# S5 powers advanced on inputs and outputs by one operation, and half of the memory's keys moved between the scan's gate and the merge

## The chip, the cores and the metric

The kernel runs on one core of one Trainium2 chip. The metric is device microseconds of one execution. A profiled execution stands beside the timed ones; its rows tell when each instruction of each engine began, how long it took and what ended the idle time before it.

## The reference, cut to what matters

Two layers of a trunk: three mixers side by side (S5, latent attention, HGRN2), their merge, attention to a memory, an FFN. x is 256 x 1024, the memory has 256 rows.

```python
h = rmsnorm(x, norm_mix[l])
(u_ssm, q_lat, kv_lat, k_rope, hg_q, hg_f, hg_i, hg_g, gate_logits) = split(h @ w_in[l])
y_ssm = s5_mixer(u_ssm, ...)        # B = ((exp(lam*step)-1)/lam) * b;  s_t = lam_bar*s_(t-1) + B u_t
                                    # y = gelu(Re(C s_t) + d*u);  z_out, z_gate = split(y @ w_glu)
                                    # return z_out * sigmoid(z_gate)
y_mla = mla_mixer(...);  y_hg = hgrn2_mixer(...)      # hgrn2 uses bounds: cumsum of softmax(hg_lb)
gates = sigmoid(gate_logits)
merged = gates[0]*y_ssm + gates[1]*y_mla + gates[2]*y_hg
x = x + merged @ w_out[l]
k, v = split(rmsnorm(mem, norm_mem[l]) @ x_w_kv[l])   # the memory's keys and values
x = x + softmax((rmsnorm(x, norm_cross[l]) @ w_q) k^T) v @ w_o
x = x + swiglu_ffn(rmsnorm(x, norm_ffn[l]))           # 1024 -> 2 x 2816 -> 1024
```

## The kernel before

Activations lie transposed, a tile of 128 rows for each of eight column groups k, with the 256 positions beside one another. Every weight chunk of up to 1 MB is fetched by SP (`raw`), then split in two for TensorE: ACT writes the rounded part `wH`, DVE the remainder `wL` (each 128x1024, two a chunk). Activations are split the same way (`h` for the input, `m` for the merged branches, `ex` for the memory, `yx` for the S5 output). Three raw buffers and four pairs of splits go round. A product is made of matmuls with wH (256 or 512 wide) and with wL.

The program is written as coroutines that a pacing loop interleaves: `LATS` says by layer how much work of a coroutine is let in beside a matmul, and `Plan` replays the whole order once, to give each tile one of the slots of `SLOTS` (t4 tiles are 4 KB a row, t2 and t1 smaller; a smaller kind may fall back on a larger slot). Each engine then runs its instructions in the fixed order that comes out, and SP its DMAs.

Five places matter.

- **Start.** `first()` makes the first input's products column group by group, with ACT and DVE splitting h and the weights as they land. POOL adds the squares for the norm beside them (L659), `col_sums` sums them over partitions, `finish` makes the row factor R, and DVE scales the four S5 inputs (`Ue`). `hg_bounds` (L669 to 693) makes the HGRN2 bounds `hb` by a chain of small DVE operations on 128x4.
- **Powers.** `s5_powers` (L816 to 852) makes the input side times lam^0..3 (`Q`) and the output side times lam^0..4 (`Pw`, `P4`), each power by six DVE operations on 128x256. Layer 0's run early in the mixers, layer 1's in layer 0's FFN.
- **S5 core.** `s5_main` (L856 to 975) does two halves: Gp and G from Q, the small matrix Tm (from tm, by DMA), products `b`, two rotations, the scan (L931), the states `X`, then y = Tm Ush + Cp X. It runs between attention heads (S, Ssb, PT, oT) and the gates (`gt`).
- **Scan to merge.** `scan(i)` makes the two halves of the gated output for 512 columns each (`zg` the gate, `zo` the value), multiplies with the branch gates (mu, Tg), and transposes Tg by TensorE (`mT`, L1415). `upd` then multiplies m with w_out and adds to x.
- **After the merge.** The memory's keys `Kc` are made from `ex` in two halves of 256 columns (`halves` makes 16 pairs of matmuls, 512 and 256 wide), followed by the query's products, which need the new x, normed and split, for all eight column groups. `drain` ends the coroutine that loads and splits the memory (`mT`, `mnat`, 0.5 MB each, L1148 and L1152; ACT squares mnat into `junk`).

Of the kernel before, what the change touches and what calls it, by code (L numbers as in the profile page):

```python
# [100 lines left out]
SLOTS = dict(t4=23, t2=10, t1=4, tn=8, tk=8, ps=8)  # L101

LEAD = 2
LATS = (0.9, 1.7)
# [13 lines left out]
class Plan:  # L118
# [40 lines left out]
def trunk(ctx, tc, A, out, plan):  # L159
# [59 lines left out]
    def tt(o, a, b, op):  # L219
        dve(o)  # L220
        DVE.tensor_tensor(out=o, in0=a, in1=b, op=op)  # L221
# [261 lines left out]
    def build_chunks(l):  # L483
        C = {}
# [28 lines left out]
        C["xk"] = [wcols(A["x_w_kv"][l], 0, 8, 256 * i, 256) for i in range(2)]  # L513
# [68 lines left out]
    def col_sums(s, ps=None):  # L582

        ps = ps if ps is not None else bank("ms")[:, 0:2]
        for tt_ in range(2):
            mm(ps[:, tt_:tt_ + 1], s[:, tt_ * 128:tt_ * 128 + 128], ones)
# [55 lines left out]
    def first(k):  # L642
# [11 lines left out]
        else:  # L654
# [14 lines left out]
    def hg_bounds():  # L669
# [3 lines left out]
        tt(lmx, gcol[:, lo:lo + 4], gcol[:, lo + 4:lo + 8], ALU.max)  # L673
# [142 lines left out]
    def s5_powers(l, bc_=None):  # L816

        ls = slice(16 * l, 16 * l + 16)
# [6 lines left out]
        S5Q[l] = (Q, Pw, P4)  # L825
        yield

        def bc(v):
            return v[:, ls].unsqueeze(2).to_broadcast([128, 16, 16])

        def cmul(o, a, b, conj=False):

            pl, mi = (ALU.subtract, ALU.add) if conj else (ALU.add, ALU.subtract)
            p1, p2 = t1([16, 16], F32, "cm"), t1([16, 16], F32, "cm")
            tt(p1, bc(a[:, 0]), b[0], ALU.mult)
            tt(p2, bc(a[:, 1]), b[1], ALU.mult)
            tt(o[0], p1, p2, mi)
            p3, p4 = t1([16, 16], F32, "cm"), t1([16, 16], F32, "cm")
            tt(p3, bc(a[:, 0]), b[1], ALU.mult)
            tt(p4, bc(a[:, 1]), b[0], ALU.mult)  # L840
            tt(o[1], p3, p4, pl)
        cmul([q[:, 3] for q in Q], coef, B)
        yield
        for k in range(1, 4):
            cmul([q[:, 3 - k] for q in Q], lam, [q[:, 4 - k] for q in Q])
            yield
        for n in range(2):
            acopy(Pw[n][:, 0], bc_[:, 2 + n], scale=-1.0 if n else None)
        yield
        for d in range(1, 5):  # L850
            cmul([q[:, d] for q in Pw] if d < 4 else P4, lam, [q[:, d - 1] for q in Pw], conj=True)
            yield

    sp = ctx.enter_context(tc.tile_pool(name="sp", bufs=1))

    def s5_main(l, Ush, out_y, heads):  # L856
        Q, Pw, P4 = S5Q.pop(l)
        gm = [cf[:, CG:CG + 1], cf[:, CG + 1:CG + 2]]
        for hf in range(2):
# [6 lines left out]
            for n in range(2):  # L866
                for g2 in range(2):
                    acopy(Gp[n][:, :, :, g2, :].rearrange("p i k h -> p k i h"), Q[n][:, :, i0:i0 + 8, :], scale=gm[g2])
# [30 lines left out]
            for i in range(8):  # L899

                for n in range(2):
                    mm(ps[0:32, 64 * i:64 * i + 64], Gp[n][:, i, 3].rearrange("p b c -> p (b c)"),
                       Pw[n][:, :, i0 + i, :], start=n == 0, stop=n == 1)
# [282 lines left out]
    def layer(l, nrm):  # L1186
# [23 lines left out]
        if l == 0:  # L1210
            nrm.sums = col_sums(sq0[0][:, 0])
# [177 lines left out]
        def scan(i):  # L1389
            zg, zo = [[bank(n) for _ in range(2)] for n in ("zg", "zo")]  # L1390

            def half(n, ps, k):
                for tt_ in range(2):
                    projB(C[n, i, k], range(2), 0, 512, ps[tt_], yHL, tt_, kbase=k, first=k == 0, last=k == 2)
# [12 lines left out]
            half("zo", zo, 2)  # L1407
            tps = [bank("mT") for _ in range(2)]
# [13 lines left out]
        ex = []  # L1422
# [226 lines left out]
```

## Time and profile before

| | us |
|---|---|
| median of 3 timed runs | 1093.5 (1093.49 to 1094.94) |
| profiled execution | 1094.6 |
| its span, first to last instruction | 1092.8 |
| TensorE busy | 1072.5 (98%) |
| VectorE (DVE) busy | 829.1 (76%) |
| ScalarE (ACT) busy | 636.4 (58%) |
| GpSimd (POOL) busy | 37.7 (3%) |
| TensorE idle while waiting for another engine | 14.0 |
| mean granted TensorE clock, as a share of full speed | 0.992 |

Busy time is the sum of an engine's instructions. TensorE is all but full, so time is to be had in its idle stretches and in the stretches where it ran at half clock; the other engines count where TensorE waits for them.

### The profile page before, as it was taken

Reading aid. Unit: us, or ns where it says so; the run is one execution under the profiler, and the core shown is the slowest. Engines: PE = TensorE matmul, PEld = TensorE weight load, DVE = VectorE, ACT = ScalarE, POOL = GpSimd, SP = SyncE. Lnnn points to the kernel's source line nnn. Section 1 sums busy time; section 2 is a strip of 40 time slices with the busy share of each in tenths; the row PEclk is TensorE's granted clock in tenths of the full one; section 3 lists DMA queues with packets and bytes.
Section 4 is the critical chain, followed back from the end, with each engine's and each line's share of the span. In section 5 each row is a group of like instructions: output and inputs, shape, how many; then the busy total and the mean of one; then the engine's idle time right before and its main releaser. Section 6 shows DMA issues by size and latency. Waiting matters only on the chain.

```text
span 1092.8 us, 16654 instructions
## 1 busy us (share of the span) xinstructions
PE 1072.5 (98%) x6416; PEld 938.0 (86%) x6416; DVE 829.1 (76%) x1438; ACT 636.4 (58%) x1050; POOL 37.7 (3%) x52
## 2 busy tenths in 40 slices
PE   8999999989899999999999999999999999999997
PEld 8999888878688888888888899888888888888887
DVE  7996777786687789986768887767677868887753
ACT  6645756855455566564565447965545566555542
POOL 4001000000000000000010001000000000000000
PEclk9999999989899999999999999999999999999999
DMA  8745552342655455655656442543474535655551
GB/s 292 214 117 178 176 163 82 116 148 85 204 167 181 133 195 193 193 183 183 188 181 186 121 136 78 191 130 108 163 233 148 197 123 167 194 191 193 174 190 61
DMA packets 145024, 179.08 MB, mean 164 GB/s; under 512 B 13553, under 2 KB 108657, under 8 KB 144945
## 3 DMA queue, kind: packets, MB, share of 16 engines
q1 hardware_dynamic: 144512, 177.45, 50.6%
q8 instruction: 50, 0.82, 0.3%
q10 hardware_dynamic: 432, 0.57, 0.2%
q14 instruction: 30, 0.24, 0.1%
HBM read 174.59 MB, written 1.05 MB: 161 GB/s over the span
## 4 chain that ended last, share of the span: by engine, by line
PE 72%; ACT 1%; DVE 0%; issue 0%; POOLq 0%; POOL 0%; ACTq 0%
PE hv L213 32%; PE dn L213 11%; PE quad L213 6%; PE gt L213 6%; PE xv L213 2%; PE ho L213 1%; PE mo L213 1%; PE lv L213 1%; PE vps L213 1%; PE zg L213 1%; PE y L213 1%; PE zo L213 1%; PE xo L213 1%; PE b L213 1%; PE xS L213 1%; PE q L213 1%
## 5 line engine op out<-in xcount | busy, mean ns | idle before, releaser
L232 ACT ACTIVATE wH<-raw 128x1024 fp32r<-128x1024 f32 (+2 forms) x332 | 340.7, 1032 | 312.7 <-PE hv L213 81.3
L221 DVE TENSOR_TENSOR wL<-raw,wH 128x1024 fp32r<-128x1024 f32 (+2 forms) x332 | 394.8, 1192 | 158.2 <-ACT wH L232 152.1
L213 PE MATMUL hv<-h,wH 128*128 128x512 f32 x848 | 298.2, 396 | 0.0
L213 PE MATMUL hv<-h,wL 128*128 128x256 f32 x848 | 236.8, 282 | 0.0
L213 PEld LDWEIGHTS hv<-h,wH 128*128 128x128 f32 x848 | 158.6, 188 | 35.3 <-issue 0.2
L213 PEld LDWEIGHTS hv<-h,wL 128*128 128x128 f32 x848 | 160.4, 189 | 1.0
L213 PE MATMUL gt<-wH,h 128*128 128x512 f32 x384 | 123.6, 402 | 0.0
L213 PEld LDWEIGHTS gt<-wH,h 128*128 128x128 f32 x384 | 70.7, 188 | 13.4
L213 PE MATMUL gt<-wL,h 128*128 128x512 f32 x192 | 75.2, 397 | 0.2 <-DVE wL L221 0.2
L213 PE MATMUL dn<-dx,wH 128*128 128x512 f32 x176 | 61.6, 394 | 0.0
L213 PE MATMUL dn<-wH,dx 128*128 128x256 f32 (+1 forms) x264 | 58.7, 319 | 0.0
L213 PE MATMUL acc<-h,wH 128*128 128x256 f32 x288 | 52.5, 284 | 0.0
L213 PE MATMUL dn<-dx,wL 128*128 128x256 f32 x176 | 49.3, 280 | 0.0
L213 PEld LDWEIGHTS dn<-wH,dx 128*128 128x128 f32 x264 | 43.6, 189 | 4.0
L213 PE MATMUL quad<-h,wH 128*128 128x512 f32 (+1 forms) x160 | 44.6, 359 | 0.5 <-ACT wH L232 0.5
L213 PEld LDWEIGHTS acc<-h,wH 128*128 128x128 f32 x288 | 44.9, 192 | 0.1
L213 PEld LDWEIGHTS gt<-wL,h 128*128 128x128 f32 x192 | 35.9, 188 | 7.5 <-DVE wL L221 0.3
L213 PE MATMUL dn<-wL,dx 128*128 128x256 f32 (+1 forms) x132 | 41.9, 319 | 0.0
L213 PE MATMUL acc<-h,wL 128*128 128x256 f32 x144 | 40.8, 284 | 0.2 <-DVE wL L221 0.2
L213 PEld LDWEIGHTS dn<-dx,wH 128*128 128x128 f32 x176 | 33.1, 188 | 7.7
L213 PE MATMUL quad<-h,wL 128*128 128x256 f32 x128 | 33.8, 292 | 2.3 <-DVE wL L221 2.1
L213 PEld LDWEIGHTS dn<-dx,wL 128*128 128x128 f32 x176 | 33.1, 188 | 0.0
(375 smaller groups left out, 2017.4 us busy)
## 6 DMA issues: line engine op xcount, KB each, us to landing
raw<-in_w_in_dram SPq DMA_DIRECT2D x48, 1024.0 KB, 5.2
raw<-in_ffn_w_gate_up_dram SPq DMA_DIRECT2D x40, 1024.0 KB, 5.1
raw<-in_ffn_w_down_dram SPq DMA_DIRECT2D x17, 1024.0 KB, 5.2
raw<-in_ssm_w_glu_dram SPq DMA_DIRECT2D x16, 512.0 KB, 3.9
raw<-in_w_out_dram SPq DMA_DIRECT2D x8, 1024.0 KB, 7.3
raw<-in_x_w_kv_dram SPq DMA_DIRECT2D x8, 1024.0 KB, 5.1
raw<-in_ffn_w_down_dram SPq DMA_DIRECT2D x6, 768.0 KB, 4.8
raw<-in_hg_w_o_dram SPq DMA_DIRECT2D x4, 1024.0 KB, 5.1
```

Source lines behind the costliest of these rows:

```text
L213: return PE.matmul(o, l, r, start=start, stop=stop)
L221: DVE.tensor_tensor(out=o, in0=a, in1=b, op=op)
L232: return ACT.activation(out=o, in_=a, func=f, **kw)
```

## The change

1. **Powers.** Q, Pw and P4 become two tiles Z of nine blocks (kind t9). Blocks 3, 2, 1, 0 hold the input side, 4 to 8 the output side. One complex product (six DVE operations of 128x256) makes block 3; three products advance both sides at once (six operations of 128x512 each); one more of 256 makes block 8. A layer has 30 DVE operations in place of 54; two small ACT copies make the signs; the copies to Cp are four in place of eight a half.
2. **Slots and pacing.** t4 has 19 slots in place of 23, t9 two; LATS of layer 0 is 1.3 in place of 0.9.
3. **Start.** The sums over partitions of the first norm are issued inside `first()`, and the first operation of `hg_bounds` is held to its place in the program, so that its chain comes after Ue.
4. **Gate and value.** The S5 output weights come in four chunks of 1 MB (each two DMAs of 0.5 MB; unit 0 the gate, unit 1 the value) in place of eight of 0.5 MB.
5. **Keys.** `keys(0)`, the first half of the memory's keys, stands in `scan(1)` behind the last zo and ahead of the transposes, with `drain()` ahead of it; its chunk is fetched ahead of w_out. `keys(1)` stays behind the merge. Both layers.

```diff
-SLOTS = dict(t4=23, t2=10, t1=4, tn=8, tk=8, ps=8)
+SLOTS = dict(t9=2, t4=19, t2=10, t1=4, tn=8, tk=8, ps=8)
-LATS = (0.9, 1.7)
+LATS = (1.3, 1.7)
...
-                        for n, c0 in (("zg", 1024), ("zo", 0)):
-                            C[n, i, k] = wcols(A["ssm_w_glu"][l], k, 2, c0 + 512 * i, 512, "one")
+                        C[part, i, k] = Chunk([wap(A["ssm_w_glu"][l], k, 2, c0 + 512 * i, 512) for c0 in (1024, 0)], 2, 1024)
+        C["xk"] = [wcols(A["x_w_kv"][l], 0, 8, 0, 256)]
         C["wo"] = [wcols(A["w_out"][l], 4 * i, 4, 0, 512, "row") for i in range(2)]
         C["wo"] += [wcols(A["w_out"][l], 0, 8, 256 * i, 256) for i in range(2, 4)]
-        C["xk"] = [wcols(A["x_w_kv"][l], 0, 8, 256 * i, 256) for i in range(2)]
+        C["xk"].append(wcols(A["x_w_kv"][l], 0, 8, 256, 256))
...
             if j == 3:
                 fold(sq0[0], POOL)
+                nrm.sums = col_sums(sq0[0][:, 0], pin=True)
...
-        tt(lmx, gcol[:, lo:lo + 4], gcol[:, lo + 4:lo + 8], ALU.max)
+        tc.keep_in_program_order(tt(lmx, gcol[:, lo:lo + 4], gcol[:, lo + 4:lo + 8], ALU.max))
...
-        Q = [t4([4, 16, 16], F32, "Q") for _ in range(2)]
-        Pw = [t4([4, 16, 16], F32, "Pw") for _ in range(2)]
-        P4 = [sp.tile([128, 16, 16], F32, tag=f"P4{n}", name=nm("P4")) for n in range(2)]
+        Z = [plan.tile(g, "t9", [128, 9, 16, 16], F32, nm("Z")) for n in range(2)]
+        sg_ = tn([2, 16])
+        acopy(sg_[:, 0], lam[:, 1, ls])
+        acopy(sg_[:, 1], lam[:, 1, ls], scale=-1.0)
...
         for k in range(1, 4):
-            cmul([q[:, 3 - k] for q in Q], lam, [q[:, 4 - k] for q in Q])
+            cmul([z_[:, 3 - k:5 + k:1 + 2 * k] for z_ in Z], lr, bc(sg_, 2), [z_[:, 4 - k:4 + k:2 * k - 1] for z_ in Z])
+            yield
+        cmul([z_[:, 8:9] for z_ in Z], bc(lam[:, 0, ls]), bc(sg_[:, 1]), [z_[:, 7:8] for z_ in Z])
-        for d in range(1, 5):
-            cmul([q[:, d] for q in Pw] if d < 4 else P4, lam, [q[:, d - 1] for q in Pw], conj=True)
...
             half("zo", zo, 2)
+            if i == 1:
+                drain()
+                keys(0)
...
         drain()
-        for i in range(2):
-            kc = Kc[:, 2 * i:2 * i + 2]
-            add_up(kc, halves(C["xk"][i], ex))
-            tt(kc, kc, Rm.unsqueeze(1).to_broadcast([128, 2, 256]), ALU.mult)
+        keys(1)
```

**Start, on DVE.** Names: h_110 to h_117 are the column groups' remainders, s and hb belong to `hg_bounds`. Before:

```order
L217 SCALAR_TENSOR_TENSOR h_112<-xp_73,gcol,h_112 128x256
L221 TENSOR_TENSOR s_359<-s_350,s_356 128x4
L217 SCALAR_TENSOR_TENSOR h_113<-xp_73,gcol,h_113 128x256
L221 TENSOR_TENSOR s_364<-s_359 128x4
L221 TENSOR_TENSOR wL_164<-raw_83,wH_163 128x512
L221 TENSOR_TENSOR s_362<-s_364,s_359 128x4
L217 SCALAR_TENSOR_TENSOR h_114<-xp_74,gcol,h_114 128x256
L217 SCALAR_TENSOR_TENSOR h_115<-xp_74,gcol,h_115 128x256
L228 TENSOR_SCALAR hb<-s_362 128x4 x2
L221 TENSOR_TENSOR wL_164<-raw_83,wH_163 128x512
```

After, on the same engine at the same place:

```order
L217 SCALAR_TENSOR_TENSOR h_112<-xp_73,gcol,h_112 128x256
L217 SCALAR_TENSOR_TENSOR h_113<-xp_73,gcol,h_113 128x256
L221 TENSOR_TENSOR wL_161<-raw_83,wH_160 128x512
L217 SCALAR_TENSOR_TENSOR h_114<-xp_74,gcol,h_114 128x256
L217 SCALAR_TENSOR_TENSOR h_115<-xp_74,gcol,h_115 128x256
L221 TENSOR_TENSOR wL_161<-raw_83,wH_160 128x512
```

The operations on 128x4 have left the row; they stand behind the four Ue.

**S5 core, second half of layer 0, on DVE**, from the rotation's last sums to the first states X. Before:

```order
L931 SCALAR_TENSOR_TENSOR w_2530<-rt_2346,w_2528 128x512
L1118 TENSOR_REDUCE s_2552<-Ssb_2551 128x1
L1119 TENSOR_REDUCE s_2552<-Ssb_2551 128x1
L931 SCALAR_TENSOR_TENSOR w_2531<-rt_2346,w_2529 128x512
L221 TENSOR_TENSOR wL_2572<-raw_2279,wH_2571 128x1024
L221 TENSOR_TENSOR w_2528<-cs_2345,w_2530 128x8x63
L221 TENSOR_TENSOR s_2556<-s_2552,lsc_1283 128x2
L221 TENSOR_TENSOR w_2529<-sn_2344,w_2531 128x8x63
L228 TENSOR_SCALAR Tg_2596<-Tg_2596 128x512
L221 TENSOR_TENSOR wL_2732<-raw_2279,wH_2731 128x1024
L228 TENSOR_SCALAR Tg_2596<-Tg_2596 128x512
L221 TENSOR_TENSOR X_2613<-w_2528,w_2529 128x8x63
```

After:

```order
L931 SCALAR_TENSOR_TENSOR w_2459<-rt_2289,w_2457 128x512
L221 TENSOR_TENSOR w_2458<-cs_2288,b_2440 128x512
L221 TENSOR_TENSOR w_2457<-cs_2288,w_2459 128x8x63
L221 TENSOR_TENSOR w_2458<-w_2458,w_2460 128x512
L931 SCALAR_TENSOR_TENSOR w_2460<-rt_2289,w_2458 128x512
L221 TENSOR_TENSOR Ssb_2562<-S_2559,cf 128x384
L221 TENSOR_TENSOR w_2458<-sn_2287,w_2460 128x8x63
L1117 TENSOR_REDUCE s_2563<-Ssb_2562 128x1
L1118 TENSOR_REDUCE s_2563<-Ssb_2562 128x1
L221 TENSOR_TENSOR X_2575<-w_2457,w_2458 128x8x63
```

Two weight splits and both Tg have left the stretch; they stand behind X now. On TensorE 57 matmuls stand between the last `b` and the first product with X, where 35 stood.

**Scan to merge, layer 0, on TensorE.** Before, from the last zo to the first product with w_out:

```order
L213 MATMUL zo_2938<-wH_2941,yx_2701 128x512
L213 MATMUL zo_2938<-wL_2942,yx_2701 128x512
L1415 MATMUL mT_3024<-ident,Tg_1712 128x128 x2
L1415 MATMUL mT_3025<-ident,Tg_1712 128x128 x2
L213 MATMUL quad_3056<-m_1500,wH_2959 128x512
```

After, where 32 matmuls of keys(0) stand in between, of which the last are shown:

```order
L213 MATMUL hv_2989<-ex_2983,wH_2929 128x512
L213 MATMUL hv_2989<-ex_2983,wL_2930 128x256
L1415 MATMUL mT_3044<-ident,Tg_1673 128x128 x2
L213 MATMUL quad_3073<-m_1487,wH_2957 128x512
L213 MATMUL quad_3073<-m_1487,wL_2958 128x256
L1415 MATMUL mT_3044<-ident,Tg_1673 128x128 x2
```

The keys' matmuls have come between the last zo and the transposes of the second half's Tg.

## Rows read from the trace of the kernel before

**Rows 1.** What TensorE waited for: us in total, times, longest

```profile
PE y L213 <- DVE X L221: 2.5, 1, 2.5
PE mT L1415 <- DVE Tg L221: 2.4, 1, 2.4
PE quad L213 <- DVE wL L221: 2.1, 1, 2.1
PE quad L213 <- DVE m L221: 1.8, 2, 1.5
PE PT L1094 <- DVE Ssb L226: 1.0, 1, 1.0
```

**Rows 2.** Stretches: length, busy by engine (instructions), granted clock, DMA share, GB/s

```profile
16.37:19.78 3.41, 3.27 (x16) 3.04 (x15) 2.58 (x7) 1.81 (x4) 0.00 (x0) 0.50 1.05 358
238.24:245.06 6.82, 5.46 (x25) 4.45 (x27) 4.60 (x15) 4.21 (x13) 0.00 (x0) 0.50 0.25 77
289.44:296.26 6.82, 5.45 (x17) 4.71 (x18) 2.15 (x4) 0.00 (x0) 0.00 (x0) 0.50 0.46 154
391.00:495.00 104.00, 104.00 (x593) 90.58 (x592) 97.84 (x165) 63.48 (x102) 0.00 (x0) 1.00 0.61 199
```

**Rows 3.** The powers' temporaries: ns min/median/max, first and last start

```profile
L221 DVE TENSOR_TENSOR cm<-lam,Pw x32: 416/419/425, 134.1 to 465.0; 128x256 f32<-128x256 f32 x32
```

**Rows 4.** DVE's timeline at the start: start, duration, tiles, [idle before]

```profile
9.13 1.28 DVE L221 TENSOR_TENSOR s<-s 128x4 f32<-128x4 f32 x1
...
14.14 0.68 DVE L221 TENSOR_TENSOR wL<-raw,wH 128x512 fp32r<-128x512 f32 x1
...
91.90 1.24 DVE L221 TENSOR_TENSOR wL<-raw,wH 128x512 fp32r<-128x512 f32 x1 [0.89 <-ACT wH L232]
```

**Rows 5.** POOL's timeline, the additions of squares

```profile
8.81 1.58 POOL L659 TENSOR_TENSOR sq<-sq,sq 128x512 f32<-128x512 f32 x1 [5.29 <-ACT sq L232]
...
91.86 0.74 POOL L577 TENSOR_TENSOR sqq<-sqq 128x256 f32<-128x256 f32 x1
```

**Rows 6.** TensorE's timeline, row factor and second weight

```profile
23.64 0.38 PE L629 MATMUL row<-ident,n 128*128 128x128 f32 x2
...
29.99 0.39 PE L213 MATMUL acc<-h,wL 128*128 128x256 f32 x1 [0.23 <-DVE wL L221]
```

**Rows 7.** DVE's timeline, scaling of the S5 inputs

```profile
24.79 2.23 DVE L221 TENSOR_TENSOR Ue<-quad,R 128x256 f32<-128x256 f32 x4
```

**Rows 8.** DVE's timeline ahead of X, second half of layer 0

```profile
235.85 1.22 DVE L221 TENSOR_TENSOR wL<-raw,wH 128x1024 fp32r<-128x1024 f32 x1
...
237.32 0.68 DVE L221 TENSOR_TENSOR X<-w,w 128x504 f32<-128x504 f32 x1
```

**Rows 9.** DMA issues from 205 to 240: times, KB, median us to landing

```profile
mnat<-in_mem_rows_dram SPq DMA_DIRECT2D x2, 512.0 KB, 4.5
mT<-in_mem_dram SPq DMA_DIRECT2D x2, 512.0 KB, 5.6
```

**Rows 10.** ACT's timeline, memory squares, then weights of the merge

```profile
242.70 1.04 ACT L232 ACTIVATE junk<-mnat 128x1024 f32<-128x1024 f32 x1
...
280.34 2.01 ACT L232 ACTIVATE wH<-raw 128x1024 fp32r<-128x1024 f32 x2 [3.87 <-DMA raw<-in_w_out_dram]
```

**Rows 11.** TensorE's timeline from the last gate product, then at the keys

```profile
282.00 0.39 PE L213 MATMUL zg<-wL,yx 128*128 128x512 f32 x1
...
316.40 0.28 PE L213 MATMUL hv<-m,wL 128*128 128x256 f32 x1
...
316.64 0.40 PE L213 MATMUL hv<-ex,wH 128*128 128x512 f32 x1
...
316.99 0.39 PE L213 MATMUL hv<-ex,wH 128*128 128x512 f32 x1
```

**Rows 12.** DVE's timeline, the last Tg, then the last split of x

```profile
287.25 0.69 DVE L221 TENSOR_TENSOR Tg<-Tg,mu 128x512 f32<-128x512 f32 x1
...
325.48 0.49 DVE L217 SCALAR_TENSOR_TENSOR h<-xp,gcol,h 128x256 fp32r<-128x256 f32 x1
```

More of the change, by code (lines that the diff above doesn't have):

```diff
@@ L220, in tt @@
         dve(o)
-        DVE.tensor_tensor(out=o, in0=a, in1=b, op=op)
+        return DVE.tensor_tensor(out=o, in0=a, in1=b, op=op)
     def ts(o, a, s1, s2=None, o0=ALU.mult, o1=None):
@@ L580, in fold, with col_sums @@
         return s[:, 0]
-    def col_sums(s, ps=None):
+    def col_sums(s, ps=None, pin=False):
         ps = ps if ps is not None else bank("ms")[:, 0:2]
         for tt_ in range(2):
-            mm(ps[:, tt_:tt_ + 1], s[:, tt_ * 128:tt_ * 128 + 128], ones)
+            m = mm(ps[:, tt_:tt_ + 1], s[:, tt_ * 128:tt_ * 128 + 128], ones)
+            if pin:
+                tc.keep_in_program_order(m)
         return ps
@@ L842, in s5_powers, with cmul @@
-        cmul([q[:, 3] for q in Q], coef, B)
+        Z = [plan.tile(g, "t9", [128, 9, 16, 16], F32, nm("Z")) for n in range(2)]
+        S5Q[l] = Z
+        sg_ = tn([2, 16])
+        acopy(sg_[:, 0], lam[:, 1, ls])
+        acopy(sg_[:, 1], lam[:, 1, ls], scale=-1.0)
+        yield
+        def cmul(o, a0, a1, b):
+            cm = [t2([512], F32, "cm")[:, 0:256 * o[0].shape[1]].rearrange("p (s i h) -> p s i h", i=16, h=16) for _ in range(4)]
+            tt(cm[0], a0, b[0], ALU.mult)
+            tt(cm[1], a1, b[1], ALU.mult)
+            tt(o[0], cm[0], cm[1], ALU.subtract)
+            tt(cm[2], a0, b[1], ALU.mult)
+            tt(cm[3], a1, b[0], ALU.mult)
+            tt(o[1], cm[2], cm[3], ALU.add)
@@ L843, in s5_powers, with bc @@
+        def bc(v, n=1):
+            return (v if n == 2 else v.unsqueeze(1)).unsqueeze(3).to_broadcast([128, n, 16, 16])
+        for n in range(2):
+            acopy(Z[n][:, 4], bc_[:, 2 + n], scale=-1.0 if n else None)
+        cmul([z_[:, 3:4] for z_ in Z], bc(coef[:, 0, ls]), bc(coef[:, 1, ls]), [b_.unsqueeze(1) for b_ in B])
         yield
+        lr = lam[:, 0, ls].unsqueeze(1).unsqueeze(3).to_broadcast([128, 2, 16, 16])
         for k in range(1, 4):
-            cmul([q[:, 3 - k] for q in Q], lam, [q[:, 4 - k] for q in Q])
+            cmul([z_[:, 3 - k:5 + k:1 + 2 * k] for z_ in Z], lr, bc(sg_, 2), [z_[:, 4 - k:4 + k:2 * k - 1] for z_ in Z])
@@ L846, in s5_powers @@
             yield
-        for n in range(2):
-            acopy(Pw[n][:, 0], bc_[:, 2 + n], scale=-1.0 if n else None)
+        cmul([z_[:, 8:9] for z_ in Z], bc(lam[:, 0, ls]), bc(sg_[:, 1]), [z_[:, 7:8] for z_ in Z])
         yield
-        for d in range(1, 5):
-            cmul([q[:, d] for q in Pw] if d < 4 else P4, lam, [q[:, d - 1] for q in Pw], conj=True)
-            yield
-    sp = ctx.enter_context(tc.tile_pool(name="sp", bufs=1))
     def s5_main(l, Ush, out_y, heads):
-        Q, Pw, P4 = S5Q.pop(l)
+        Z = S5Q.pop(l)
@@ L867, in s5_main @@
                 for g2 in range(2):
[L868 removed]
+                    acopy(Gp[n][:, :, :, g2, :].rearrange("p i k h -> p k i h"), Z[n][:, 0:4, i0:i0 + 8, :], scale=gm[g2])
             yield
@@ L902, in s5_main @@
                     mm(ps[0:32, 64 * i:64 * i + 64], Gp[n][:, i, 3].rearrange("p b c -> p (b c)"),
-                       Pw[n][:, :, i0 + i, :], start=n == 0, stop=n == 1)
+                       Z[n][:, 4:8, i0 + i, :], start=n == 0, stop=n == 1)
             for g2 in range(2):
@@ L1393, in half @@
                 for tt_ in range(2):
-                    projB(C[n, i, k], range(2), 0, 512, ps[tt_], yHL, tt_, kbase=k, first=k == 0, last=k == 2)
+                    projB(C["zo", i, k], range(2), 512 * (n == "zo"), 512, ps[tt_], yHL, tt_, kbase=k, first=k == 0, last=k == 2)
             half("zg", zg, 0)
@@ L1420, in scan, with keys @@
                     split(mx_[k][:, 0], mx_[k][:, 1], two(tps[q])[:, o])
-        ex = []
+        ex, Kc = [], []
+        def keys(i):
+            hs = halves(C["xk"][i], ex)
+            if i == 0:
+                Kc.extend((t4([4, 256], F32, "Kc"), t1([256], F32, "Rm")))
+                row_of(rmc, Kc[1])
+            kc = Kc[0][:, 2 * i:2 * i + 2]
+            add_up(kc, hs)
+            tt(kc, kc, Kc[1].unsqueeze(1).to_broadcast([128, 2, 256]), ALU.mult)
         for part in ORDER:
```

24 lines of the change are left out of this document (3 added, 21 removed).

## Prediction

> **What bounds the kernel now.** I read the list of TensorE's waits first. TensorE is busy 98% of the span and idle for another engine during 14.0 us, and five waits make most of that: 2.5 for the states X, 2.4 for Tg, 2.1 for a remainder wL at the start, 1.8 for the merged m, 1.0 for an attention tile [rows 1]. Then the table of stretches: the granted clock is 0.50 of full, the 1.2 GHz level, in three stretches of 3.41, 6.82 and 6.82 us, and each begins behind one of the waits above 2 us [rows 2]. Matmuls there take twice as long, so a stretch costs half its length: 1.7, 3.4 and 3.4, together 8.5. So three places hold about 20 us: the start (2.1 and 1.7, 3.8 in all), the S5 core's second half (2.5, a small wait of 0.3, 1.0 and 3.4, 7.2), and the step from scan to merge in layer 0 (2.4, 1.5 and 3.4, 7.3). Elsewhere TensorE does not wait, and what another engine saves there gives nothing.
>
> **Powers.** Before, 54 operations of 0.42 us a layer, 22.7 [rows 3]. After, 12 of these and 18 of 512 columns at 0.68 [rows 8]: 5.0 + 12.2 = 17.3. That is 5.4 us a layer less on DVE, and on the path I cost it at nothing: layer 1's powers run in layer 0's FFN, where DVE is busy 97.8 of 104 us and TensorE all of them [rows 2], and layer 0's run beside the mixers (the first of the row at 134), where none of the waits above lies. What hides them is the products. Without that cover the saving would be at most 5.4 a layer.
>
> **Start.** The 128x4 operation at 9.13 takes 1.28 us and ends at 10.41 [rows 4]; POOL's addition of 8.81 ends at 10.39 [rows 5]. It is tiny, and was held. Is it the tiny operation that POOL holds, or whichever comes next? At 91.90 a wL of the usual 0.68 takes 1.24 and ends at 93.14, beside an addition of POOL from 91.86 to 92.60 [rows 4, 5]. So the hold falls on any DVE operation that begins inside an addition. The Trainium skill, GPSIMD Engine Reference, section 1 Specifications, says that GpSimd shares its SBUF interfaces with VectorE and contends with VectorE instructions that have two SBUF inputs, which wL and h are; it speaks against this part of the change, and by it the holds stay. POOL's four additions stay in place, so I let the hold pass to the next h or wL. What is gained is that a wL no longer stands behind both a held operation and the h behind it: the fourth column group's wL, 14.14 to 14.82 [rows 4], comes at about 13.0, with TensorE ready at 12.8, and the next group's at 15.9, where TensorE is ready at 14.8. The wait of 2.1 becomes about 0.4 and 1.2, with no single one of 2 us, and I take the slow clock to be gone: 0.6 + 1.7 = 2.3 gained. Against it: the row factor's transposes come eight groups of three matmuls later (0.35 a group, as long as a pair [rows 11]), 2.9 us behind the end of the first product. Ue began 1.15 behind them and takes 2.23 [rows 6, 7], and now stands ahead of the weight remainder that before began behind it in time. With 1.22 for that wL [rows 8] and 0.4 of small operations it is ready some 7.7 us behind the product's end, and TensorE wants it after 17 groups and the transposes, 6.2: 1.5 of waiting where 0.2 was [rows 6], so 1.3 lost. **Net -1.0.** Bounds: +0.7 if the slow clock stays, -2.5 if Ue is hidden.
>
> **S5 core, second half.** The 14 DVE operations from the first rotation to X take, by their lengths, eight at 0.68, two scans at 1.22 (as long as a wL) and 1.6 for four small ones: 9.4 [rows 8]. Both weight splits and Tg, 3.3 us, are behind X now. TensorE has 57 matmuls there; 48 are 512 wide at 0.235 (two thirds of the 0.35 that a pair takes [rows 11]) and nine short ones about 0.1: 12.2. X is in time by some 2 us, and wait and slow clock go: -7.2. What is late next? First the tile PT of the next head: it needs ACT's scaling, which now stands behind two wH. I take 1.6, between 0 and 2.5 (two wH of 1.0 and the scaling; half of the 2.01 of two wH [rows 10]). Second, the memory. With 19 slots, mT's second half and mnat wait for the last y; before, they waited only for products ahead of it. They land 4.5 to 5.6 behind their issue [rows 9]. On ACT two squares of mnat at 1.04 [rows 10], two splits of yx, a wH and a copy of PT wait behind them: 5.5 + 4.15 = 9.65 us behind the last y. TensorE has 9.9 us of mo and zg until it needs that PT. I take 0.4, between 0 and 2. **Net -5.2.** Bounds -7.2 and -2.7 without a new slow stretch.
>
> **Scan to merge.** Before, the last gate product ended at 282.39 [rows 11], Tg at 287.94 [rows 12]: 5.5 us, with ACT having waited 3.87 for w_out [rows 10]. TensorE had only zo to do. After, zo (1.9) and 16 pairs of keys(0) (16 x 0.35 = 5.6) stand there with eight transposes (0.5): 8.0. The wait for Tg goes, with 2.5 us over, and the wait for m also, since eight pairs of the first half's m go ahead of the second's. Both gone with their clock: 7.3. Chunks of 1 MB let the three raw buffers reach further, so I let w_out and the keys' chunk land in time; if not, the bound is the 3.87 [rows 10] less the 2.5 over, 1.4. **Net -6.8.**
>
> **After the merge, both layers.** The last product with w_out began at 316.40, the last split of x ended at 325.97 [rows 11, 12], 9.3 us behind that product, and both halves of the keys (11.3) covered it. Now one half is left, 5.6, and six or seven groups of the query's products, 2.4: 8.0. The first half's adds are gone from DVE, so the lag falls to about 8.6. I take 0.5 a layer, between 0 and 1.3. **+1.0 in all.** Layer 1's two small waits at its merge, 0.3 each, go: **-0.6**.
>
> **Sum.** -1.0 - 5.2 - 6.8 + 1.0 - 0.6 = -12.6. On the profiled execution that is 1094.6 - 12.6 = 1082.0. It lay 1.1 above the median, so the median base gives 1080.9; new pacing in layer 0 reorders everything between 30 and 230, where small waits may come, and I stay at 1082.
>
> **The rivals.**
>
> *The memory's rows are late.* Place: ACT behind the last y. The margin is 0.25 us; each further microsecond of landing is one of TensorE's. If the three half-megabytes land at 8 us, as three that share the queue may, the wait is 2.3 and the clock falls for 6.8: 2.3 + 3.4 - 0.4, so 1087.3. For it: all three are now issued together. Against it: nothing else is on the DMA then.
>
> *The keys don't cover.* Their own chunk stands ahead of w_out in the queue, and if it is late, TensorE waits as before, only earlier: 2.4 and 3.4 come back, 1087.8. For it: ACT waited 3.87 for w_out [rows 10]. Against it: deeper reach.
>
> *All of it is hidden.* Start, PT and the norm without new waits: -2.5 - 7.2 - 6.8 - 0.6, so 1077 on the profiled base, 1076 on the median's.
>
> *Slower: the norm is bared in both layers.* Place: between keys(1) and the query's last column groups, with w_out's adds and x's split on DVE behind weight remainders. If the order puts three more wL of 1.22 ahead of that split than I count, the lag is 12.2, the wait 4.2 a layer, and with the clock's 3.4, 7.6 a layer, 15.2 in two: 1082 - 1.0 + 15.2 = 1096.2. It decides against the change from about 3.8 us of waiting a layer on. For it: DVE does all of add, split and weights there. Against it: only 9.3 before, with more work on it. A wait of 2.1 to 3.7 a layer gives 1092 to 1095, no change to be seen.
>
> *The holds go with the tiny operations.* If POOL holds only those, the fourth wL is free at 12.3 and the start gains 3.8 less 1.3: 1080.5, inside my own range.
>
> **How the numbers follow.** Forecast (with the last rival) 0.52, 1079 to 1086. All hidden 0.09. Memory late 0.13, keys late 0.08, both giving 1086 to 1091. No change, by the norm's smaller wait or by several of these, 0.10; slower 0.08. A measurement of this kernel can tell about 0.2%, 2.2 us, from no change. Faster: 0.52 + 0.09 + 0.13 + 0.08 = 0.82. Range 1075 to 1091.5, which leaves out the last two cases.
>
> **What would show it.** In the waits of TensorE, X and Tg are gone or below 1 us; PT waits for ACT by 1 to 2 us near 240, oT or zo by less than 1. No stretch at half clock near 240 and near 290. At the start, wL or h of some 1.2 us beside POOL's additions, two waits below 1.5, and a new one of about 1.5 at the second weight behind Ue. In both layers a wait for h below 1.3 some 8 us behind the merge. The prediction is wrong if a wait above 2 us with a slow stretch stands anywhere in layer 0, or if the holds are gone.

## The result, and the profile after

The changed kernel takes 1082.7 us (median of 4 runs, 1082.46 to 1082.86) beside 1093.95 for the kernel before in the same comparison (1093.49 to 1094.94): a ratio of 0.9896, interval 0.9879 to 0.9913, or 11.3 us less. The forecast was 1082.0. The number came out; the ledger behind it did not in all its lines, and the forecast's own sign of being wrong came true in one place (below).

The list of TensorE's waits after (us in total, times, longest) answers [rows 1]:

```profile
PE ho L213 <- ACT hox L232: 2.7, 1, 2.7
PE quad L213 <- DVE wL L221: 1.9, 2, 1.2
PE rope L213 <- ACT qraw L232: 1.8, 1, 1.8
PE acc L213 <- DVE wL L221: 1.1, 1, 1.1
...
PE oT L213 <- ACT PT L232: 0.7, 1, 0.7
```

X, Tg, m and Ssb are gone from the list. `quad` is now two waits, and `acc` behind Ue has grown from 0.2 to 1.1, both as forecast. At the top, though, stand two waits that the forecast had nowhere: `ho` for hox, the split of HGRN2's output, and `rope` for qraw, the copy of the raw query. In all TensorE is idle 10.5 us where it was 14.0.

The table of stretches after answers [rows 2] (columns as there):

```profile
186.85:190.26 3.41, 3.41 (x10) 2.36 (x9) 3.41 (x9) 1.82 (x6) 0.00 (x0) 0.50 0.66 190
391.00:495.00 104.00, 104.00 (x597) 90.85 (x596) 93.42 (x142) 61.81 (x98) 0.00 (x0) 1.00 0.58 189
```

The three slow stretches of before are gone, 17.05 us in length. One of 3.41 us is left, at a new place, behind the wait for hox. In the FFN, where layer 1's powers run, DVE's busy time fell from 97.8 to 93.4 with TensorE full in both: 4.4 us of DVE gave nothing there. The powers are 2.8 of these: the trace before has 48 of their operations a layer (96 in two layers; the list of the change and the forecast say 54) and 20.1 us in layer 1, the trace after 30 and 17.3.

The ledger from last product to last product (1086.49 before, 1074.76 after, -11.7): waits -3.5, half of the slow stretches (17.05 - 3.41) / 2 = -6.8 by the forecast's rule, and -1.4 in many small pieces that I don't assign. TensorE's timeline before, two products inside the last slow stretch:

```profile
292.23 0.63 PE L213 MATMUL quad<-m,wH 128*128 128x512 f32 x1
...
292.87 0.63 PE L213 MATMUL quad<-m,wH 128*128 128x512 f32 x1
```

The rule of half the length is an upper bound. A pair of products takes 0.64 us here and 0.35 at full clock [rows 11], 1.8 times as long and not twice, and TensorE idles inside the stretches too (it is busy 5.46 and 5.45 of 6.82 [rows 2]). By busy time the stretches cost some 6.4 before and 1.5 after, -4.8, and 3.4 of the gain stay unassigned. The sums below keep the forecast's rule.

**Start.** DVE's timeline after, then POOL's (start, duration, tiles, [idle before]), beside [rows 4, 5]:

```profile
9.09 1.43 DVE L221 TENSOR_TENSOR wL<-raw,wH 128x512 fp32r<-128x512 f32 x1 [0.28 <-ACT wH L232]
...
12.88 2.38 DVE L217 SCALAR_TENSOR_TENSOR h<-xp,gcol,h 128x256 fp32r<-128x256 f32 x2
```

```profile
8.62 1.35 POOL L661 TENSOR_TENSOR sq<-sq,sq 128x512 f32<-128x512 f32 x1 [5.10 <-ACT sq L232]
...
12.37 1.74 POOL L661 TENSOR_TENSOR sq<-sq,sq 128x512 f32<-128x512 f32 x1 [0.30 <-ACT sq L232]
```

The hold has passed to a wL (1.43 in place of 0.68) and to pairs of h (2.38 a pair here; 0.87 where POOL is idle, as an experiment below shows), each beside an addition of POOL. TensorE's timeline, the second weight behind Ue, beside [rows 6]:

```profile
28.75 0.39 PE L213 MATMUL acc<-h,wL 128*128 128x256 f32 x1 [1.14 <-DVE wL L221]
```

It begins at 28.75 in place of 29.99: 1.24 earlier, with the wait of 1.14 in front of it.

**S5 core, second half.** DVE's, ACT's and TensorE's timelines, then the issues of the memory's rows (KB each, median us to landing), beside [rows 8 to 10]:

```profile
238.21 0.68 DVE L221 TENSOR_TENSOR X<-w,w 128x504 f32<-128x504 f32 x1
...
253.40 1.06 ACT L232 ACTIVATE junk<-mnat 128x1024 f32<-128x1024 f32 x1 [2.71 <-DMA mnat<-in_mem_rows_dram]
...
257.25 0.49 ACT L232 ACTIVATE PT<-PT 128x384 f32<-128x384 f32 x1
...
241.23 0.43 PE L213 MATMUL y<-Cp,X 128*64 128x128 f32 x2
...
257.80 0.92 PE L213 MATMUL oT<-PT,Vp 128*128 128x256 f32 x4 [0.74 <-ACT PT L232]
```

```profile
mnat<-in_mem_rows_dram SPq DMA_DIRECT2D x2, 512.0 KB, 6.5
```

The second X ends at 238.89 and TensorE comes to it at 241.23, 2.3 us later. The memory's rows take 6.5 us to land, ACT's squares wait for them, the copy of PT stands behind, and TensorE waits 0.74.

**Scan to merge, and behind it.** TensorE's timeline, the last zo, a pair of the second half's transposes, then the last product with w_out and the first of the query, beside [rows 11]; and DVE's, the last Tg and the last split of x, beside [rows 12]:

```profile
282.12 0.40 PE L213 MATMUL zo<-wL,yx 128*128 128x512 f32 x1
...
288.84 0.38 PE L1415 MATMUL mT<-ident,Tg 128*128 128x128 f32 x2
...
312.41 0.28 PE L213 MATMUL hv<-m,wL 128*128 128x256 f32 x1
...
318.17 0.39 PE L213 MATMUL hv<-h,wH 128*128 128x512 f32 x1
...
286.89 0.68 DVE L221 TENSOR_TENSOR Tg<-Tg,mu 128x512 f32<-128x512 f32 x1
...
318.69 0.49 DVE L217 SCALAR_TENSOR_TENSOR h<-xp,gcol,h 128x256 fp32r<-128x256 f32 x1
```

Tg is ready at 287.57, and TensorE asks for it at 288.84: keys lie between the last zo and there. Nothing waits behind the merge either. The last split of x ends at 319.18, 6.5 us behind the end of the last product with w_out (9.3 before, 8.6 forecast).

**The two waits that nobody ordered.** ACT's timeline ahead of qraw, then ahead of hox, and TensorE's two rows:

```profile
107.79 1.33 ACT L232 ACTIVATE Gp<-Z,cf 128x512 f32<-128x512 f32 x2
...
109.41 1.28 ACT L232 ACT_TABLE_LOAD   x1
...
111.35 2.00 ACT L232 ACTIVATE Kh<-kraw 32x1024 f32<-32x1024 f32 x2
113.38 0.38 ACT L232 ACTIVATE qraw<-qp 128x256 f32<-128x256 f32 x1
...
180.51 1.34 ACT L232 ACTIVATE Gp<-Z,cf 128x512 f32<-128x512 f32 x2 [7.69 <-PE y L213]
...
182.23 1.32 ACT L232 ACTIVATE Gp<-Z,cf 128x512 f32<-128x512 f32 x2
...
185.54 0.62 ACT L232 ACTIVATE hox<-osb 128x512 fp32r<-128x512 f32 x1
```

```profile
113.81 0.70 PE L213 MATMUL rope<-qraw,cf 128*128 128x256 f32 x2 [1.76 <-ACT qraw L232]
...
186.22 2.11 PE L213 MATMUL ho<-wH,hox 128*128 128x512 f32 x5 [2.71 <-ACT hox L232]
```

In both, ACT makes Gp, the masked copies of the powers, ahead of something that TensorE needs at once. The first of layer 0's Gp copies begins at 96.4 after, at 133.3 before: the powers' input side is done earlier (at 96.3, before at 134.2), so its copies came earlier in ACT's order. Ahead of qraw they are not alone. The table load of 1.28 us and `sn` of 0.63 behind it, factors of S5's rotation, ran at 79.4 and 80.7 before and came later, into this place; Kh stands there too. Which of these operations made the wait of 1.76 is not shown. That it is ACT's order is shown by the experiments on the three waits and on the first half's Gp.

### The profile page after: what moved, and what is told of

Its sections match the earlier page's. It is cut to its first block, busy times and chain, and to the rows that moved or that the text cites. A ratio compares the mean times of both kernels' runs of the same rounds, so it can differ in the third digit from the quotient of the medians.

```text
span 1081.1 us, 16609 instructions
## 1 busy us (share of the span) xinstructions
PE 1064.2 (98%) x6416; PEld 933.0 (86%) x6416; DVE 827.2 (77%) x1402; ACT 637.8 (59%) x1040; POOL 37.7 (3%) x52
## 3 DMA queue, kind: packets, MB, share of 16 engines
HBM read 174.59 MB, written 1.05 MB: 162 GB/s over the span
## 4 chain that ended last, share of the span: by engine, by line
PE 95%; ACT 3%; DMA 1%; DVE 0%; issue 0%; SPq 0%; POOLq 0%; POOL 0%; ACTq 0%
PE hv L213 33%; PE gt L213 12%; PE dn L213 11%; PE quad L213 7%; PE acc L213 5%; PE ho L213 2%; PE zo L213 2%; PE vps L213 2%; PE lv L213 2%; PE zg L213 2%; PE xv L213 2%; PE y L213 2%; PE mo L213 1%; PE b L213 1%; PE q L213 1%; PE oT L213 1%
```

## The experiments

All differences are to the kernel before in the same comparison; one of two variants is the difference of their ratios, times 1094.

### Undoing one part

**Keys back behind the merge.**

```diff
-            if i == 1:
-                drain()
-                keys(0)
...
+        keys(0)
         keys(1)
```

> The changed kernel with both halves of the memory's keys behind the merge again, and their chunks fetched behind w_out; all else stays. Theory (the keys' products cover DVE's chain to Tg and m): the waits for Tg and m come back at 1.5 to 2.5 and about 1 us, with a slow stretch of 6.8, so 4 to 7 us slower than the changed kernel, 1087 to 1090. Rival (the gate's chunks of 1 MB alone, which let the weights come earlier, had removed the waits): at most 1 us slower, no slow stretch near 285.

1088.4 us, ratio 0.9956 (0.9943 to 0.9969): 6.6 us slower than the changed kernel by the ratios. The waits come back, as TensorE's timeline shows:

```profile
286.16 0.50 PE L213 MATMUL quad<-m,wH 128*128 128x512 f32 x1 [2.10 <-DVE m L221]
```

With 0.56 for Tg, 1.37 (in place of 0.74) for PT and two waits of 0.3 in layer 1, that is 3.9 us of waiting more; the other 1.7 of the 5.6 at the last product I don't assign. The slow clock did not come: no slow stretch follows that wait of 2.1. The keys are the cover, and without them the price is idle time here.

**Eight chunks of 0.5 MB for gate and value.**

```diff
-                        C[part, i, k] = Chunk([wap(A["ssm_w_glu"][l], k, 2, c0 + 512 * i, 512) for c0 in (1024, 0)], 2, 1024)
+                        for n, c0 in (("zg", 1024), ("zo", 0)):
+                            C[n, i, k] = wcols(A["ssm_w_glu"][l], k, 2, c0 + 512 * i, 512, "one")
```

> The changed kernel with the gate and value weights in eight chunks of 0.5 MB again. Theory (the keys cover, the chunks only shift landings): 0 to 1.5 us slower, no wait above 1 us between the scan and the merge. Rival (the deeper reach of the raw buffers is needed, w_out or the keys' chunk lands late): a wait of 2 us or more for a weight near 283, with a slow stretch, 4 to 6 us slower.

1083.2 us, ratio 0.991 (0.988 to 0.994): no difference from the changed kernel that these intervals can tell, and in the traces the last products end 0.2 us apart (1074.55 and 1074.76). With the keys in place no gain of the chunks is to be seen.

**The old start.**

```diff
-                nrm.sums = col_sums(sq0[0][:, 0], pin=True)
...
-        tc.keep_in_program_order(tt(lmx, gcol[:, lo:lo + 4], gcol[:, lo + 4:lo + 8], ALU.max))
+        tt(lmx, gcol[:, lo:lo + 4], gcol[:, lo + 4:lo + 8], ALU.max)
...
+        if l == 0:
+            nrm.sums = col_sums(sq0[0][:, 0])
```

> The changed kernel with the bounds' small operations and the norm's sums where they stood before. Theory (POOL's additions hold whatever DVE begins, so the small operations cost little of their own, and what the edit gained is the slow clock less a new wait behind Ue): the wait of 2.1 and the slow stretch of 3.4 come back, the wait of 1.1 at the second weight goes, and the second weight's product begins 1.2 us later than in the changed kernel; 0.5 to 1.5 us slower in all. Rival (the edit freed DVE of 3.8 us of holds): 3 us slower or more.

1082.3 us, ratio 0.9898 (0.9868 to 0.9929): no difference either. Yet the wait of 2.1 and its slow stretch are back, TensorE's timeline and the table of stretches say, and TensorE is 0.9 later at the wait for qraw (112.97, where the changed kernel has 112.05):

```profile
14.78 0.96 PE L213 MATMUL quad<-h,wL 128*128 128x256 f32 x3 [2.10 <-DVE wL L221]
...
257.80 0.81 PE L213 MATMUL oT<-PT,Vp 128*128 128x256 f32 x4
```

```profile
14.86:18.27 3.41, 3.41 (x16) 3.41 (x17) 3.41 (x6) 2.01 (x2) 0.45 (x1) 0.50 1.06 377
```

The row of 257.80 tells where the microsecond went: oT begins at 257.80 in both kernels, with a wait of 0.74 there in the changed one and none here. The memory's rows land at the same time in both (ACT's first square at 253.33 and 253.40), although the first of the memory's loads is issued 0.80 later here (247.26 and 246.46). So the landing took that much longer in the changed kernel, and its lead was lost there. Why it took longer is not known, and it is no rule: without the keys the load is issued at 246.49 and the first square comes at 254.09, and an experiment below carries a gain of 2 us past this wait.

**The old powers**, with t4 at 23 slots and the pace of the list left at 1.3.

> The changed kernel with the powers as before (54 operations of 256 columns a layer, 23 slots of the large kind, copies to Cp in two parts). Theory (the shorter powers let the S5 core run ahead: this took X out of TensorE's way in the second half, and put the copies to Gp ahead of the attention's and HGRN's copies, the new waits of 1.8 and 2.7): the wait for X comes back with 2 us and a slow stretch, 5 to 7 us, and the two new waits with their 1.7 of slow clock go, 6 us; so 2 us faster to 3 slower. Rival (pacing or the keys made the cover for X, the powers nothing): X stays without a wait and the new waits stay too, within 1 us of the changed kernel.

1094.9 us, ratio 1.0017 (1.0002 to 1.0031): 13 us slower, all of the gain and more. But the reason is another than the old wait for X, which is 0.87 here. TensorE's timeline, then the DMA issues from 205 to 250:

```profile
245.18 0.66 PE L213 MATMUL y<-Tm,Ush 128*64 128x128 f32 x2 [7.10 <-DMA Tm<-To]
```

```profile
Tm<-To SPq DMA_DIRECT2D x1, 128.0 KB, 10.6
```

Tm's small transfers were issued behind weights and a memory load and took 10.6 us to land (2.9 in the changed kernel). In all TensorE waits 16.0 us in place of 10.5, and slow stretches before the end make 17.1 us in place of 3.4: by half their length that is the 12.3 between the last products. The run had changed the order of the transfers along with the powers, so it could not price the powers. The next run does, together with their slots, which are undone in both runs; powers and slots are not told apart.

**The old powers at the old pace**: the same, and

```diff
-LATS = (1.3, 1.7)
+LATS = (0.9, 1.7)
```

> The changed kernel with the powers undone (one operation for each half, four to a block and side, and the old four-column slots) and the pace of the list at .9, as in the kernel before. The earlier run with the powers undone kept the pace of 1.3 and came out 12 us slower than the changed kernel, with a wait of 7.1 us for Tm at 238. Theory: that wait was the pace's and the transfers' order; at .9 the wait of y for X is back at 2 to 2.5 us with one slow stretch behind it, and the time is 4 to 8 us above the changed kernel, 1086 to 1091. Rival 1: the powers are worth the whole 12 us at either pace, so 1093 or above. Rival 2: the powers are worth nothing and the pace was all: within 2 us of the changed kernel, 1081 to 1085.

1084.9 us, ratio 0.9927 (0.9912 to 0.9942): 3.4 us slower than the changed kernel by the ratios, 2.0 by the last product in the two traces. That is between my theory (4 to 8) and the rival (2 at most). TensorE's timeline and the stretch behind:

```profile
237.01 0.66 PE L213 MATMUL y<-Cp,X 128*64 128x128 f32 x2 [2.49 <-DVE X L221]
...
239.41 0.69 PE L1097 MATMUL PT<-ident,Ssb 128*128 128x128 f32 x2 [1.05 <-DVE Ssb L226]
```

```profile
236.93:243.75 6.82, 5.47 (x24) 4.48 (x26) 4.78 (x15) 4.04 (x12) 0.00 (x0) 0.50 0.46 155
```

X and Ssb wait to the hundredth as before, and the slow stretch is as long [rows 1, 2]: the powers, with their slots, removed these, 2.5 + 1.05 + 3.4 = 6.9. But `rope`, `ho` with its slow stretch, and oT wait for nothing here: 1.76 + 2.71 + 1.7 + 0.74 = 6.9. So what the powers gained in the second half of the S5 core was given back at the new waits of the changed kernel. The 2.0 us left at the last product are nearly all small waits: 0.47, 0.27, 0.23 and 0.16, which the changed kernel has not, and 0.65 more for the first weight at 6.9, a wait that runs from 0.16 to 1.28 over the kernels here and is hardly the powers'.

**The changed kernel at pace 0.9.** The same line of LATS alone.

> The changed kernel with layer 0's pacing at 0.9 as before. Theory (the shorter powers move the S5 core ahead, whatever the pacing): the new waits for the query's copy near 112 and for HGRN's split near 184 stay, 1.8 and 2.7 with a slow stretch, X is in time; within 2 us of the changed kernel. Rival (the pacing of 1.3 made the new waits, or made X's cover): these waits go, 4 to 6 us faster, or X's wait comes back, 5 us slower.

1081.8 us, ratio 0.9902 (0.9885 to 0.9918): the pace gives nothing with the new powers. The wait of 1.76 for qraw is there at this pace as well and missing with the old powers at either pace, so it comes with the powers. The one of 2.71 for hox is not there: three of 0.4 to 0.6, for POOL and DVE, stand in its place, and the old powers at pace 1.3 wait 1.47 for hox. So that one hangs on the pace too. TensorE's timeline and the stretch:

```profile
183.37 1.97 PE L631 MATMUL ro<-ident,s 128*128 128x128 f32 x8 [0.51 <-POOL s L250]
```

```profile
183.07:186.48 3.41, 2.82 (x12) 2.42 (x12) 3.38 (x9) 1.95 (x4) 0.24 (x1) 0.50 0.00 0
```

The slow stretch came with no more than this wait of 0.51 us, inside which it begins.

**Start and chunks alone**: old powers, pace 0.9, both halves of the keys behind the merge.

> The start's new order and the 1 MB chunks alone: the powers as in the kernel before, the pace at .9, and both halves of the keys behind the merge. Theory (the forecast's terms): the start is worth 1.0 us, the chunks nothing, and all else is back: X 2.5 with its slow stretch, Tg 2.4, m 1.5 and theirs; so 1.0 under the kernel before, 1092 to 1094, two slow stretches of 6.82 us, none at the start. Rival: the start's gain needs the rest of the change to reach the end, or is larger than its waits say: the same as before within 0.5 us, or 1090 and less.

1090.0 us, ratio 0.9974 (0.9964 to 0.9985): 2.8 us under the kernel before, where I had expected 1.0. TensorE's timeline from the last zo, and the two slow stretches:

```profile
284.87 0.66 PE L1415 MATMUL mT<-ident,Tg 128*128 128x128 f32 x4 [0.74 <-DVE Tg L221]
...
287.69 0.76 PE L213 MATMUL quad<-m,wH 128*128 128x512 f32 x1 [1.46 <-DVE m L221]
```

```profile
236.38:243.21 6.83, 4.98 (x20) 3.99 (x21) 5.28 (x16) 3.55 (x10) 0.00 (x0) 0.50 0.47 155
287.58:290.99 3.41, 3.30 (x10) 2.85 (x11) 0.89 (x2) 0.00 (x0) 0.00 (x0) 0.50 0.80 253
```

Here the chunks work: Tg waits 0.74 in place of 2.36, since w_out no longer comes late for ACT (3.87 of waiting before [rows 10], none here), and the slow stretch at the merge has half its length. The chunks and the keys work on the same wait: the chunks alone take off part of it, and beside the keys no gain of theirs is to be seen (second experiment).

The kernels in a row, each with one part more:

| kernel | us | ratio to before | us under before | step |
|---|---|---|---|---|
| before | 1093.95 | 1 | 0 | |
| start and chunks | 1090.0 | 0.9974 | 2.8 | -2.8 |
| and keys | 1084.9 | 0.9927 | 8.0 | -5.1 |
| and powers, with their slots | 1081.8 | 0.9902 | 10.7 | -2.7 |
| and pace 1.3 (the change) | 1082.7 | 0.9896 | 11.4 | -0.7 |

The intervals are 1.2 to 1.9 us each way, so the last step is no difference, and that of the powers is barely clear of it.

### Taking away the costs that are left

**POOL's additions on DVE.**

```diff
-                POOL.tensor_tensor(out=sq0[0], in0=sq0[0], in1=s, op=ALU.add)
+                DVE.tensor_tensor(out=sq0[0], in0=sq0[0], in1=s, op=ALU.add)
...
-                fold(sq0[0], POOL)
+                fold(sq0[0], DVE)
```

> The changed kernel with the four additions of squares at the start on DVE in place of POOL, no other. Theory (POOL's additions hold any DVE operation that begins beside them): DVE's splits there take 0.68 and 0.48 each again, nearly 4 us of holds go for 2.5 us of additions, the two waits for weight remainders (0.7 and 1.2) shrink to 1.2 or less together, and the row factor comes no later. At 112 us the kernel stands 0.5 to 1.5 ahead; at the end 0 to 1. Rival (only tiny operations are held, and these are gone from there): DVE has 2.5 us more to do, the waits grow by 1 us or more.

1080.1 us, ratio 0.9883 (0.9866 to 0.9901), 1.4 by the ratios and 2.5 by the medians under the changed kernel. DVE's timeline:

```profile
9.38 0.68 DVE L221 TENSOR_TENSOR wL<-raw,wH 128x512 fp32r<-128x512 f32 x1
9.98 0.87 DVE L217 SCALAR_TENSOR_TENSOR h<-xp,gcol,h 128x256 fp32r<-128x256 f32 x2
```

0.68 and 0.87, where the changed kernel has 1.43 and 1.91: the holds came from POOL, and though DVE does four operations more, both waits of the start are gone and the wait behind Ue falls to 0.90. The Trainium skill, GPSIMD Engine Reference, section 1 Specifications, which the forecast weighed, tells of contention between GpSimd and VectorE instructions with two SBUF inputs. These rows agree with it. TensorE's timeline at the wait for PT:

```profile
255.53 0.92 PE L213 MATMUL oT<-PT,Vp 128*128 128x256 f32 x4 [0.58 <-ACT PT L232]
```

This gain passes the wait for the memory's rows: TensorE is 2.0 us ahead of the changed kernel at the wait for qraw (111.79), the first of the memory's loads is issued 2.1 earlier (244.35), oT begins 2.3 earlier, and the last product ends 2.6 earlier.

**Three waits.** The copy of qraw is put ahead in priority; the Gp copies of layer 0's second half are pinned in program order, behind hox; mnat is loaded ahead of mT's second half.

```diff
-            acopy(qraw, pp[:, 0:256])
+            with tc.high_priority(offset=HP):
+                acopy(qraw, pp[:, 0:256])
...
+                    if hf == 1 and l == 0:
+                        tc.keep_in_program_order(m)
...
+            if q == 0:
+                nat.extend(t4([1024], F32, "mnat") for _ in range(2))
...
```

> The changed kernel with three orders altered: the copy of the raw query given priority on ACT, the second half's Gp copies held to their place in the program (behind HGRN's split), and the memory's rows loaded ahead of the second half of its transpose. Theory (the new waits are matters of order on ACT and SP): the wait near 112 falls from 1.8 below 1, that near 184 from 2.7 to 1 or so and its slow stretch goes, and that for the tile PT near 257 (0.7) goes; 4 to 6 us faster than the changed kernel, 1076.5 to 1078.5. Rival (the Gp copies come so late that X is late again): a wait of 2 us or more for X or Tm near 240, and no gain or a loss.

1078.8 us, ratio 0.9873 (0.9859 to 0.9888), 2.5 by the ratios and 3.9 by the medians under the changed kernel, a little less than expected. No slow stretch is left before the end, `ho` falls to 1.17, oT waits no more (mnat lands in 3.8 us in place of 6.5). qraw waits no more either, with the first half's Gp left where it was. But there another operation behind ACT's queue is late. TensorE's timeline:

```profile
115.66 0.74 PE L213 MATMUL gt<-wH,h 128*128 128x512 f32 x2 [1.50 <-ACT wH L232]
```

**Squares and three waits together.** The two edits above.

> The changed kernel with both sets of edits: the four additions of the start (three of squares and the fold of wL's halves) on VectorE in place of GpSimd, and the three placements of the experiment before (qraw's copy put ahead, the Gp copies behind hox, mnat's rows loaded ahead of the second mT). Theory: the costs lie at different places, and each placement gives what it gave alone: 2.5 us of the start and 3.9 us of the three waits, so 1082.7 - 6.4 = 1076.3, with no slow stretch before the end and idle time of TensorE of about 6 us in all. Rival: what the start gains is given back at the next wait on a transfer (the MLP's weights or the memory's rows), as with the old start: then the time stays at that of the three placements, 1078.8.

1077.9 us, ratio 0.9861 (0.9847 to 0.9876), 1.6 more than expected. The waits are down to 6.0 us as expected, but a slow stretch of 3.42 us (1.7 lost) follows the wait for the gate's weight.

**The same, with the old start** (that edit as above).

> As the run before it (squares on VectorE and the three placements), with the start's order of the kernel before (hg_bounds and col_sums as there). Theory of the forecast: the start's new order is worth 0.9 to 1.2 us, which the changed kernel gave back at the wait for the memory's rows; since these rows are loaded earlier here, nothing gives it back, and this run is slower than the run before it by 1 to 3 us (more if the slow stretch behind the 2.1 us wait at 12.7 comes back). Rival: the old order loses only through GpSimd's additions, which are gone in both: then the two agree within 0.7 us.

1079.05 us, ratio 0.987 (0.9849 to 0.989), against 0.9861: the intervals overlap. The medians have the old start 1.2 slower, the traces 0.5 faster (the last products end at 1070.24 and 1070.70), so the times can't tell the theory from the rival. The waits speak for the rival: without POOL's additions the old order waits 0.22 and 0.37 at the start and the new one 0.90 behind Ue.

**The first half's Gp copies pinned as well.**

```diff
-                    if hf == 1 and l == 0:
+                    if l == 0:
                         tc.keep_in_program_order(m)
```

> As the run with squares on VectorE and the three placements, with the first half's Gp copies of layer 0 pinned in program order as well, so that on ScalarE two pairs of 1.33 us leave the stretch ahead of the gates' weights at 112 and come some 16 operations later; two operations of the forget gate pass ahead of the weights instead (0.4 us each behind the one before). Theory: the wait of 1.5 us for a weight at 112 and the slow stretch of 3.41 us behind it are ScalarE's queue, so both go and 1.5 + 1.7 = 3.2 us are gained, 1074.7. Rival: the copies come too late for the first half's products (a new wait of 1 us or more between 115 and 180), and the time stays at 1077 to 1079.

1076.3 us, ratio 0.9842 (0.9825 to 0.986): the best of all, 17 us under the kernel before, though only 1.6 of the 3.2 us expected of this edit came. ACT's timeline, then TensorE's, and the stretch:

```profile
134.96 1.94 ACT L232 ACTIVATE Gp<-Z,cf 128x512 f32<-128x512 f32 x3
```

```profile
105.03 0.73 PE L213 MATMUL gt<-wH,h 128*128 128x512 f32 x2 [0.64 <-ACT Qh L232]
...
181.42 1.44 PE L213 MATMUL ho<-wH,hox 128*128 128x512 f32 x4 [1.17 <-ACT hox L232]
```

```profile
183.32:186.74 3.42, 3.42 (x12) 2.85 (x11) 3.42 (x10) 1.05 (x3) 0.00 (x0) 0.50 0.80 291
```

The Gp copies now run at 135, when nobody waits for ACT, and the wait at 112 is gone (0.64 at 104 is new). That shows whose queue it was. The slow stretch has moved behind the wait for hox, the same 1.17 that was followed by none in the three kernels before.

## Why the prediction was right, point by point

**Powers: nothing on the path.** This step failed. Its count was wrong (48 operations a layer before, so 2.8 us of DVE saved and not 5.4), without harm: in the FFN it gave nothing, as forecast. What the step left out is that the order on the engines behind changes with the powers: ACT's Gp copies moved from 133 to 96 and on, ahead of hox in the second half, and Gp, a table load, `sn` and Kh came ahead of qraw. Cost: 1.76 + 2.71 + 1.7 = 6.2 at the pace of 1.3; at 0.9 the waits there are 1.76 + 1.5 with a slow stretch of the same length. The text said that new small waits might come between 30 and 230 and priced none. It also named a sign of being wrong: a wait above 2 us with a slow stretch anywhere in layer 0. The wait of 2.71 for hox is one.

**Start: net -1.0.** Measured 1.24 earlier at the second weight; the waits forecast as 0.4, 1.2 and 1.5 are 0.73, 1.21 and 1.14 (the terms of the last add up to 7.9 and not 7.7, so it should have read 1.7); no slow stretch; the holds passed on. Set beside the old start, though, none of it reached the end of the changed kernel: in these two traces the lead of 0.9 was lost where the memory's rows took longer to land, for a reason not known.

**S5 core: -5.2.** The X wait with its stretch went, X being ready 2.3 us ahead (2 forecast). With the old powers at the old pace it is back, so the powers with their slots do it. PT waited 0 where I took 1.6, and the memory's rows 0.74 where I took 0.4 (landing 6.5, forecast 5.5). Together -7.2 + 0.7 = -6.5.

**Scan to merge: -6.8.** Measured -7.3: both waits and the stretch gone, keys(0) in time. That the keys do it is shown by the first experiment; that the chunks do part of it alone, by the last of the first group. I let the chunks matter only as a margin, which is what they are beside the keys.

**After the merge: +1.0.** Measured 0: the lag was 6.5 and not 8.6. I had taken off only the first half's adds to Kc. In DVE's order two weight remainders stand in that stretch where three and part of a fourth stood, and one addition of squares, one add to x and one to Kc less, which makes the 2.8 us under the 9.3 of before. The slower rival, the bared norm, assumed three remainders more; there was one fewer, and no wait at all.

**Layer 1: -0.6.** As measured.

The sum by these: -1.2 - 6.5 - 7.3 + 0 - 0.6 = -15.6, and the two new waits with their stretch +6.2: -9.4, beside -10.3 in waits and clock and -11.7 at the last product. So the forecast of -12.6 on the profiled base stands near the result by luck in part: an unpriced loss of 6.2 met three terms that came out better (1.3, 0.5 and 1.0) and some 2.3 of gains in small pieces, more if the slow clock costs less than half a stretch. The mechanisms were right at the start, in the S5 core and at the merge; the step that failed is the powers', costed at nothing on the path.

## What to carry to other kernels

Work that is made faster upstream changes the next engine's order (here Gp came forward from 133 to 96, and `sn` back from 81 to 111); look at which critical operation on that engine now stands behind it, and hold the other one to its place. Two edits that work on the same wait must be priced together, since the weaker shows its worth only without the stronger. And a wait for a transfer can swallow a gain ahead of it: from the issue of the first of the memory's loads to ACT's first square it was 6.0 to 7.6 us in five kernels, a spread larger than the start's gain.

## What the runs showed of the hardware that I had not expected

The slow clock does not follow from the length of the wait in front of it alone. Behind 2.10 us with the keys undone, at 286, there was none; behind 2.10 us at the start, with the old start, one of 3.41; behind 0.51 (pace 0.9, at 183), among small transposes, one of 3.41; behind one and the same 1.17 none in three kernels and one in a fourth. With the old powers at pace 1.3 one came with no wait in front of it, while TensorE went over from 64- and 1-wide products to 512-wide ones:

```profile
170.84:174.25 3.41, 3.41 (x10) 2.63 (x9) 3.41 (x6) 1.06 (x1) 2.48 (x1) 0.50 0.06 23
```

It also differs between runs of one kernel: the four timed runs of the best version are 1075.57 twice and 1077.01 and 1077.07, with a mean granted clock of 0.999 in the first two and 0.998 in the others, and half a stretch of 3.41 would be 1.7 us. That this is the reason is not shown. I had taken the slow clock as certain behind waits above 2 us. In a forecast it is better set down as a chance, at each place where TensorE waits or runs short matmuls, of 1.7 or 3.4 us.
